# Weight pieces that begin at a different place in their tiles every four pieces

## The chip, the cores and the metric

The kernel runs on one core of a Trainium2 chip. The metric is device time in microseconds (us), median of the runs shown.

## What is computed

The reference is two transformer blocks, one behind the other, on one sequence of 256 tokens with a width of 2048, all in float32. The first block has compressed, selected and windowed attention beside a convolution branch, an output projection and a feed-forward layer with a short convolution. The second has latent attention beside gated linear attention, an output projection, and a gated feed-forward layer, with its scales and shifts from a conditioning vector (adaLN). Cut to its frame:

```python
h = rms_norm(x, mix_norm_g[l])
proj = h @ w_in[l]
...
x = x + jnp.concatenate([attn, conv], axis=-1) @ w_out[l]
h = rms_norm(x, ffn_norm_g[l])
x = x + conv_glu_ffn(h, w_up[l], ffn_conv_w[l], ffn_conv_b[l], w_down[l])
```

Nearly all of the work is activations times weight matrices, with few tokens (256) and some 380 MB of weights that are each used once.

## The kernel before

The weights lie packed in HBM in the order of their use and are cut into 740 pieces, of 128 partitions by up to 1024 elements. `load_raw` brings two pieces at a time into a tile `raw`. Each piece is then split in two, so that TensorE can multiply in its faster float32r form without losing precision: `split_h` (line 456) has ScalarE (ACT) copy the piece to a float32r tile `wh`, the high part; `split_l` (line 463) has VectorE (DVE) write what the rounding left out, `raw - wh`, to a tile `wl`, the low part. There are four buffers of `wh` (LA + 1) and three of `wl` (LA), each 1024 elements long per partition, and both parts begin at the first element of their tile. The activations are held as high and low parts too (`X`, `hid`, `o`, `oh`/`ol`, `ch`/`cl` and others).

`run_group` goes through 119 groups of pieces in a fixed order. In a group of mode `w`, for each of (mostly) four tiles of output columns and each row block k, three matmuls follow each other: `wh` slice with the high activations, the same `wh` slice with the low ones, `wl` slice with the high ones. Here the weights are the stationary operand (128 x 128) and the activations stream through (256 columns; 258 in some matmuls of four groups). A piece gives 24 such matmuls. In a group of mode `x` (114 of the pieces: `vv`, `uv`, `vg`, and the `g` groups, the second block's down projection) the weights stream, with 512 columns, and 128 x 128 of the activations are stationary; a piece gives 12 matmuls. In all there are 16,344 matmuls on weights: 1,368 with 512 columns, 512 with 258, and 14,464 with 256. Each has a weight load of its own.

The work on the side (attention, norms, evacuations, the adaLN sums that are named `ac`) is put between these matmuls by a planner with a model of the engines' time (`tick`, `need`, `Clock`). SP issues the loads, `load_raw` at the end of each tile's `split_l`, when the tile is used up.

Where operands begin: a slice of a weight piece begins a multiple of 128 elements (512 bytes) behind its tile's begin (in `gt` a multiple of 48 elements). `rows` (line 707) puts the activations' rows at a fixed distance of 4 elements (PHASE) behind their tile's begin, with row lengths of 384 (XROW) or 256 elements. In the built program the tiles `wh`, `wl`, `X`, `hid`, `o` and `ch` begin at the same address modulo 512 bytes. So, modulo 512 bytes, the rows of `X`, `hid` and `o` begin 16 bytes behind the weight slices, always. Other activations differ: `ch` has no PHASE and begins 0 bytes behind, `cl` 32 bytes behind, and the heads of `oh` (a tile each, 1,056 bytes apart) begin 16, 48, 80, ... bytes behind, those of `ol` 272, 304, ....

Of the kernel before, what the change touches and what calls it, by code (L numbers as in the profile page):

```python
# [14 lines left out]
F32R = mybir.dt.float32r  # L15
# [13 lines left out]
LA = 3  # L29
# [259 lines left out]
def halves(i, n):  # L289

    return ((0, n // 2), (n // 2, n)) if i == 0 else ((0, n),)


class Engine:


# [76 lines left out]
class Kern:  # L373
# [81 lines left out]

    def split_h(self, i):
        m = MCS[i]
        h = self.wp.tile([128, 1024], F32R, name="wh", bufs=LA + 1)
        for a, b in halves(i, m["len"]):
            self.act(h[:, a:b], self.raws[m["tile"]][:, m["o"] + a:m["o"] + b], AF.Copy)  # L460
        self.hl[i] = h

    def split_l(self, i):
        m = MCS[i]
        n, h = m["len"], self.hl[i]
        l = self.wp.tile([128, 1024], F32R, name="wl", bufs=LA)
        for a, b in halves(i, n):
            self.tt(l[:, a:b], self.raws[m["tile"]][:, m["o"] + a:m["o"] + b], h[:, a:b].bitcast(F32), OP.subtract)
        self.hl[i] = (h, l)
        if i == len(MCS) - 1 or MCS[i + 1]["tile"] != m["tile"]:  # L470
            self.raws.pop(m["tile"])
            self.used = m["tile"] + 1
            self.load_raw(self.used + RAW)
# [1555 lines left out]
```

## Time and profile before

| | |
|---|---|
| median of 3 runs | 2261.15 us (2258.84 to 2265.59) |
| profiled execution | 2265.83 us |
| its span, first to last instruction | 2263.9 us |
| TensorE matmul busy (PE) | 2234.7 us, 99% |
| TensorE weight load busy (PEld) | 2137.7 us, 94% |
| VectorE (DVE) / ScalarE (ACT) busy | 1698.5 us, 75% / 1187.7 us, 52% |
| mean granted TensorE clock | 0.996 |

A matmul's recorded time covers its way through the array, so that two or three overlap: 281 ns for one that has 256 columns, while the next one starts some 115 ns behind it. The busy share therefore says little. What counts is the cadence: the time from one matmul's start to the next one's start. The timeline gives the starts to 10 ns, so that a stretch of many matmuls, divided by their number, gives the cadence to a fraction of a nanosecond.

### The profile page before, as it was taken

The page shows a single profiled execution, that of the slowest core. Times are in us where ns is not written, and L with a number is a line of the kernel's source. Part 1 is how long each engine was busy: PE and PEld are TensorE (multiplying, and loading weights), DVE is VectorE, ACT ScalarE, POOL GpSimd, SP SyncE. Part 2 cuts the span into 40 slices and gives each one's busy share as a digit, 9 for nine tenths or more (in the row PEclk, how much of TensorE's full clock was granted, in tenths as well). Part 3 has the DMA queues.
Part 4 walks back from the last instruction along what each step waited for, and adds up shares of the span by engine and source line. Part 5 has one row for each costly group of instructions (what it writes and reads, how often), then busy time and mean ns, then how long its engine had stood idle before and what let it go on. Part 6 is the DMA issues. An engine that isn't in the chain of part 4 may idle for free.

```text
span 2263.9 us, 42338 instructions
## 1 busy us (share of the span) xinstructions
PE 2234.7 (99%) x17486; PEld 2137.7 (94%) x17486; DVE 1698.5 (75%) x2632; ACT 1187.7 (52%) x1826; POOL 4.9 (0%) x16
## 2 busy tenths in 40 slices
PE   8999999999999999999999999999999999999997
PEld 8998889999999999999999889989998999889996
DVE  7999888898987788888879876577665665544455
ACT  5447776655553355555556664555444444444443
POOL 0000000000000000000000000000000000000000
PEclk9999999999999999999999999999999999999999
DMA  6544325688888787877756644546666665555553
GB/s 242 186 166 159 127 80 193 239 293 301 303 287 308 294 297 284 301 291 290 251 204 225 214 153 148 193 149 215 241 239 231 246 236 192 187 183 171 187 186 130
DMA packets 89089, 499.22 MB, mean 221 GB/s; under 512 B 9904, under 2 KB 12352, under 8 KB 42432
## 3 DMA queue, kind: packets, MB, share of 16 engines
q1 hardware_dynamic: 88896, 496.51, 61.7%
q8 instruction: 137, 2.24, 0.4%
q14 instruction: 56, 0.46, 0.1%
HBM read 494.35 MB, written 2.12 MB: 219 GB/s over the span
## 4 chain that ended last, share of the span: by engine, by line
PE 93%; DVE 4%; ACT 2%; issue 1%; DMA 1%; SPq 0%; DVEq 0%; ACTq 0%
PE ps L305 93%; DVE wl L305 1%; DMA raw<-in_wst_dram 1%; DVE cacc L305 0%; ACT wh L305 0%; DVE og L305 0%; ACT P L305 0%; DVE X L305 0%; ACT X L305 0%; ACT L305 0%; DVE ss L305 0%; DVE blk L305 0%; ACT y L305 0%; ACT vt L305 0%; DVE XT L305 0%
## 5 line engine op out<-in xcount | busy, mean ns | idle before, releaser
L305 PE MATMUL ps<-X,wh 128*128 128x256 f32 (+1 forms) x7680 | 1374.8, 281 | 3.6 <-ACT X L305 2.9
L305 ACT ACTIVATE wh<-raw 128x1024 fp32r<-128x1024 f32 (+2 forms) x741 | 781.5, 1056 | 875.6 <-PE ps L305 798.8
L305 DVE TENSOR_TENSOR wl<-raw,wh 128x1024 fp32r<-128x1024 f32 (+2 forms) x741 | 898.5, 1216 | 451.4 <-PE ps L305 381.3
L305 PEld LDWEIGHTS ps<-X,wh 128*128 128x128 f32 x7680 | 1174.5, 188 | 12.3 <-issue 5.8
L305 PE MATMUL ps<-X,wl 128*128 128x256 f32 (+1 forms) x3840 | 1073.8, 280 | 3.4 <-DVE wl L305 3.4
L305 PEld LDWEIGHTS ps<-X,wl 128*128 128x128 f32 x3840 | 721.3, 188 | 4.0 <-DVE wl L305 4.0
L305 DVE SCALAR_TENSOR_TENSOR ac<-wa,cs,ac 128x512 f32<-128x512 f32 x360 | 269.6, 749 | 6.4
L305 PE MATMUL ps<-hid,wh 128*128 128x256 f32 x1408 | 247.8, 279 | 0.0
L305 PE MATMUL ps<-wh,hid 128*128 128x512 f32 x704 | 220.1, 394 | 0.0
L305 PEld LDWEIGHTS ps<-hid,wh 128*128 128x128 f32 x1408 | 214.1, 188 | 1.2 <-issue 1.2
L305 PE MATMUL ps<-hid,wl 128*128 128x256 f32 x704 | 196.0, 278 | 0.0
L305 PEld LDWEIGHTS ps<-wh,hid 128*128 128x128 f32 x704 | 131.7, 188 | 29.2 <-issue 0.2
L305 PE MATMUL ps<-wl,hid 128*128 128x512 f32 x352 | 138.1, 392 | 0.0
L305 PEld LDWEIGHTS ps<-hid,wl 128*128 128x128 f32 x704 | 132.2, 188 | 0.0
L305 DVE SCALAR_TENSOR_TENSOR cacc<-upad,cat,cacc 128x256 f32<-128x256 f32 x240 | 99.7, 478 | 0.3 <-ACT cacc L305 0.2
L305 PEld LDWEIGHTS ps<-wl,hid 128*128 128x128 f32 x352 | 67.1, 191 | 15.7
L305 DVE SCALAR_TENSOR_TENSOR y<-vt,fv,y 128x256 f32<-128x256 f32 x176 | 73.4, 479 | 0.0
L305 PE MATMUL ps<-wh,X 128*128 128x512 f32 x192 | 62.0, 404 | 0.0
L305 PE MATMUL ps<-o,wh 128*128 128x256 f32 x256 | 48.9, 290 | 1.2 <-ACT o L305 1.1
L305 ACT ACTIVATE y<-ps,fv 128x256 f32<-128x256 f32 x84 | 49.0, 583 | 0.0
L305 ACT ACT_TABLE_LOAD x30 | 38.5, 1283 | 10.8 <-DMA XT<-in_x_dram 4.5
L305 PEld LDWEIGHTS ps<-wh,X 128*128 128x128 f32 x192 | 35.4, 189 | 7.3
(319 smaller groups left out, 1754.8 us busy)
## 6 DMA issues: line engine op xcount, KB each, us to landing
raw<-in_wst_dram SPq DMA_DIRECT2D x363, 1024.0 KB, 4.9
wa<-in_wada_dram SPq DMA_DIRECT2D x176, 512.0 KB, 6.2
wa<-in_wada_dram SPq DMA_DIRECT2D x32, 256.0 KB, 5.5
raw<-in_wst_dram SPq DMA_DIRECT2D x4, 768.0 KB, 4.4
raw<-in_wst_dram SPq DMA_DIRECT2D x4, 512.0 KB, 6.3
B<-dtab SPq DMA_DIRECT2D x8, 256.0 KB, 5.2
out_dram<-og SPq DMA_DIRECT2D x8, 256.0 KB, 2.8
XT<-in_x_dram SPq DMA_DIRECT2D x3, 512.0 KB, 7.5
```

Source lines behind the costliest of these rows:

```text
L305: return f(*x, **k)
```

## The change

A function `places` gives each piece two distances, one for its high part and one for its low part. The tiles `wh` and `wl` become 128 elements longer, and the part begins that many elements behind the tile's begin. Nothing else is changed: not the instructions, their shapes, their order in the program's text, the buffers' number or the loads.

```diff
+def places(i):
+    n = i // 4
+    a, b = (4 * n % 128,) * 2 if n < 64 else (36 * n % 128, 4 * (n * n // 3 + n) % 128)
+    return (a + 2, b + 2) if n % 4 == 3 and n >= 32 else (a, b)
...
     def split_h(self, i):
         m = MCS[i]
-        h = self.wp.tile([128, 1024], F32R, name="wh", bufs=LA + 1)
+        h = self.wp.tile([128, 1024 + 128], F32R, name="wh", bufs=LA + 1)[:, places(i)[0]:]
...
     def split_l(self, i):
...
-        l = self.wp.tile([128, 1024], F32R, name="wl", bufs=LA)
+        l = self.wp.tile([128, 1024 + 128], F32R, name="wl", bufs=LA)[:, places(i)[1]:]
```

Worked out: for the first 256 pieces (n below 64) both parts begin 4n elements (16n bytes) behind, modulo 128 elements, so that all 32 steps of 16 bytes are gone through twice. From then on the high part goes in steps of 36 elements (144 bytes) and the low part in growing ones, so that the two are mostly apart. In every fourth set of four from n = 35 on (152 pieces of the 740) 2 elements (8 bytes) are added to both; all other distances are multiples of 16 bytes.

## Rows read from the trace of the kernel before

**Rows 1.** The page: busy us (share of the span) xinstructions; granted clock in 40 slices.

```profile
PE 2234.7 (99%) x17486; PEld 2137.7 (94%) x17486; DVE 1698.5 (75%) x2632; ACT 1187.7 (52%) x1826; POOL 4.9 (0%) x16
...
PEclk9999999999999999999999999999999999999999
```

**Rows 2.** The page: the chain of work that ended last, share of the span.

```profile
PE 93%; DVE 4%; ACT 2%; issue 1%; DMA 1%; SPq 0%; DVEq 0%; ACTq 0%
```

**Rows 3.** The page's groups: xcount | busy us, mean ns | idle before, releaser.

```profile
L305 PE MATMUL ps<-X,wh 128*128 128x256 f32 (+1 forms) x7680 | 1374.8, 281 | 3.6 <-ACT X L305 2.9
L305 ACT ACTIVATE wh<-raw 128x1024 fp32r<-128x1024 f32 (+2 forms) x741 | 781.5, 1056 | 875.6 <-PE ps L305 798.8
L305 DVE TENSOR_TENSOR wl<-raw,wh 128x1024 fp32r<-128x1024 f32 (+2 forms) x741 | 898.5, 1216 | 451.4 <-PE ps L305 381.3
...
L305 PE MATMUL ps<-wh,hid 128*128 128x512 f32 x704 | 220.1, 394 | 0.0
```

**Rows 4.** Waits: engine, line, releaser: us in total, times, longest us.

```profile
ACT wh L305 <- PE ps L305: 798.8, 525, 5.7
...
DVE wl L305 <- PE ps L305: 381.3, 286, 4.0
```

**Rows 5.** Stretches without side matmuls: us, PE, PEld, DVE, ACT, POOL busy (xcount), clock, DMA.

```profile
410.00:440.00 30.00, 30.00 (x255) 30.00 (x254) 27.32 (x50) 19.52 (x29) 0.00 (x0) 1.00 0.62 228
...
865.00:885.00 20.00, 20.00 (x174) 20.00 (x173) 19.69 (x28) 11.39 (x17) 0.00 (x0) 1.00 0.78 289
...
1010.00:1035.00 25.00, 25.00 (x223) 25.00 (x222) 22.65 (x31) 13.74 (x20) 0.00 (x0) 1.00 0.81 297
1060.00:1080.00 20.00, 20.00 (x174) 20.00 (x173) 18.66 (x25) 10.94 (x16) 0.00 (x0) 1.00 0.76 277
...
1570.00:1600.00 30.00, 30.00 (x255) 30.00 (x254) 19.19 (x23) 12.97 (x17) 0.00 (x0) 1.00 0.73 267
...
1900.00:1930.00 30.00, 30.00 (x260) 30.00 (x259) 14.45 (x14) 12.19 (x14) 0.00 (x0) 1.00 0.57 202
2110.00:2140.00 30.00, 30.00 (x256) 30.00 (x254) 15.29 (x15) 13.27 (x15) 0.00 (x0) 1.00 0.52 179
```

**Rows 6.** The same view, two stretches in which the weights stream (512 columns).

```profile
1940.00:2000.00 60.00, 60.00 (x259) 48.59 (x258) 29.32 (x27) 22.34 (x21) 0.00 (x0) 1.00 0.55 186
2180.00:2250.00 70.00, 70.00 (x311) 57.98 (x310) 37.58 (x37) 30.12 (x38) 0.00 (x0) 1.00 0.44 151
```

**Rows 7.** Timeline of PE at a break by side work: start us, us, what.

```profile
1041.05 0.42 PE L305 MATMUL ps<-ac,vecs 128*32 128x128 f32 x8
```

**Rows 8.** Timeline: first matmuls of group oz0 and, 384 later, of group u0_0.

```profile
349.06 0.28 PE L305 MATMUL ps<-ch,wh 128*128 128x256 f32 x1
...
394.00 0.40 PE L305 MATMUL ps<-X,wh 128*128 128x256 f32 x2
```

**Rows 9.** Timeline, groups o2_1 and o2_2: starts of four runs of 96 matmuls.

```profile
1423.13 0.28 PE L305 MATMUL ps<-oh,wh 128*128 128x256 f32 x1
...
1434.40 0.40 PE L305 MATMUL ps<-X,wh 128*128 128x256 f32 x2
...
1445.80 0.28 PE L305 MATMUL ps<-oh,wh 128*128 128x256 f32 x1
...
1457.07 0.40 PE L305 MATMUL ps<-X,wh 128*128 128x256 f32 x2
```

**Rows 10.** Timeline, group z1: two stretches, of 36 and of 69 matmuls.

```profile
1174.18 0.40 PE L305 MATMUL ps<-X,wh 128*128 128x258 f32 x2
...
1178.34 0.40 PE L305 MATMUL ps<-X,wh 128*128 128x258 f32 x2
...
1187.11 0.42 PE L305 MATMUL ps<-X,wh 128*128 128x258 f32 x2
...
1195.70 0.41 PE L305 MATMUL ps<-X,wh 128*128 128x258 f32 x2
```

**Rows 11.** The tile upad: xcount: ns min/median/max, first and last start.

```profile
L305 DVE SCALAR_TENSOR_TENSOR cacc<-upad,cat,cacc x240: 463/478/485, 45.6 to 308.2; 128x256 f32<-128x256 f32 x120
```

## What the change should do to the time

> **What bounds the kernel.** Read the page first. PE is busy for 2234.7 us, 99% of the span, at the full granted clock (2.4 GHz) in all 40 slices [rows 1], and the chain that ended last is PE for 93% [rows 2]. So no other engine counts on its own; the question is how densely the matmuls follow each other. The two engines that split the weights are not the bound: in the waits ACT stands 798.8 us before `wh` and DVE 381.3 us before `wl`, both for PE to give a buffer free [rows 4]. They run ahead and are held back.
>
> The view on which all else rests is the table by stage [rows 5, 6]: stretches in which only matmuls on weights run. A count there includes the matmuls that were in flight at the opening, so the cadence is the stretch plus one matmul's recorded 0.28 us (0.39 us with 512 columns [rows 3]), over the count. For 256 columns: 30.28/255 = 118.7 ns from 410 us on and again from 1570 us, 20.28/174 = 116.6 from 865 and from 1060, 30.28/260 = 116.5 from 1900, 25.28/223 = 113.4 from 1010, 30.28/256 = 118.3 from 2110 [rows 5]. With 512 columns: 60.39/259 = 233.2 and 70.39/311 = 226.3 [rows 6]. Same shapes, same clock, same relation of the operands' begins (16 bytes), and yet three cadences, each held for tens of us. It doesn't follow the load of DVE, ACT or the DMA: at 410 and at 865 us DVE is busy for 27.32 of 30 and for 19.69 of 20 us, while the 118.3 at 2110 us goes with 15.29 of 30. It changes where the stream is broken: the 113.4 ends at 1041.05 us, where eight short `ac` matmuls of the side work come in [rows 7], and from there it is 116.6. So TensorE's stream has several steady cadences, and a disturbance chooses among them.
>
> The average that the change has to beat: going through the timeline, the undisturbed stretches of 256 columns have 118.7 ns for some 620 us, 116.6 for 750, 113.4 for 36. (620 x 118.7 + 750 x 116.6 + 36 x 113.4) / 1406 = 117.4 ns. One nanosecond more or less on all 14,464 such matmuls is 14.5 us.
>
> **What the change adds and takes away.** No instruction, byte, wait or buffer is added or taken away; the program's order is the same, since the planner's costs depend on shapes. What moves is where `wh` and `wl` begin, and with that the relation to the activations' begin, which was 16 bytes for nearly all matmuls.
>
> *The splits.* ACT's copy (1056 ns) and DVE's subtraction (1216 ns) [rows 3] now write, and DVE reads `wh`, at another begin. The nearest row: the convolution's 31 taps read `upad` at begins one element apart, and take 463 to 485 ns [rows 11]. Taken for nothing; if it were all of those 22 ns, 740 splits would cost DVE 16 us, under the 381.3 us in which it waits for PE [rows 4]. Were that cover gone, the weight load of the next piece would be late by the 22 ns, once in 24 matmuls (0.9 ns each, 13 us in all).
>
> *The matmuls.* Does the begin matter at all? Two places of the trace show matmuls with other relations. Group `oz` has 0 bytes for two of each three matmuls and 32 for the third: 384 matmuls from 349.06 to 394.00 us, 44.94/384 = 117.0 ns [rows 8]. The `o2` groups go through eight heads with relations of 16, 48, 80, ... and 272, 304, ... bytes, and then through 96 matmuls on `X` with 16 bytes: (1434.40 - 1423.13)/96 = 117.4 ns, then 11.40/96 = 118.8, then in the next group 11.27/96 = 117.4 again [rows 9]. Here the cadence changes at once, without a break, as the operand's begin does. So the relation does matter, by about 1 ns, and other relations than 16 bytes gave 117.0 and 117.4, where 16 bytes give 117.4 on average. Put together evenly, (117.0 + 117.4 + 117.4)/3 = 117.3: I take -0.1 ns, or 14,464 x -0.1 = -1.4 us. As bounds I keep the 113.4 ns everywhere, 14,464 x (113.4 - 117.4) = -58 us, and the 118.7 ns everywhere, 14,464 x 1.3 = +19 us. (In the trace only the activations' begin varies, not the weights'; that the relation counts, and not one side alone, is an assumption.)
>
> *The streaming groups.* 1,368 matmuls: 28 of the 114 pieces (the last four groups) have 226.3 ns, nearly all others 233.2, a mean of (28 x 226.3 + 86 x 233.2)/114 = 231.5 ns. All at 233.2 is +2.3 us, all at 226.3 is -7.1 us; taken for nothing.
>
> *The half steps.* In 152 of 740 pieces the begin is 8 bytes off a 16-byte step, which no matmul on weights shows before. The nearest is a row of 258 columns, which ends on such a half step: 4.16 us/36 = 115.6 ns at its quicker cadence [rows 10], against 113.4 for 256 [rows 5]. A column costs (233.2 - 116.6)/256 = 0.46 ns, so two cost 0.9 and 1.3 ns are left over. On 152/740 of 14,464 matmuls, 2,971, that is +4 us; bounds are the steady cadences again, as for any other place. I take a quarter of it, +1 us, since only the first element of each slice is off, and not the length.
>
> Sum: -1.4 + 1 = about -0.5 us on the profiled execution: 2265.83 to 2265.3 (its span of 2263.9 and 1.9 around it). That execution lies 0.2% over the median of 2261.15, so the forecast for the median is 2260.5 us.
>
> *What the skill says.* The Trainium skill, page "TensorE: Matmul & The Clock Gate", section "Step-by-step: what each phase is for", says that PE reads the streaming operand and the weights through two independent SBUF ports, so that loading the next weights takes nothing from the running matmul. By that, in the groups where the weights are stationary, their place would change nothing: 2261 us. The trace doesn't settle it, since only the streaming operand's begin varies in it; it is why a part of the middle case's chance is for no effect at all.
>
> **The rivals.**
> *Other places find the quick cadence.* For it: 113.4 ns exists with these operands [rows 5], and a break can lead into it; a new relation every four pieces is a break without lost time. Against: the runs with other relations [rows 8, 9] didn't fall into it. If a quarter of the matmuls ran at 113.4 and the rest as before, 14,464/4 x 4.0 = -14.5 us: 2247 us.
> *Other places push the stream to 118.7 ns, or worse.* The mechanism is the same, in the other direction: at begins where the two reads get in each other's way the stream settles at a long cadence, and with a new begin every 96 matmuls no good one is kept. For it: a far longer cadence exists, in `z1`, 8.59 us/69 = 124.5 ns beside 115.6 for the same matmuls [rows 10]; 16 bytes may be a good relation among bad ones. Against: again [rows 8, 9], at or below the average. All at 118.7 and 233.2 is +19 + 2.3 us: 2282; a quarter of the matmuls at 124.5 would be 14,464/4 x 7.1 = +26 us, 2287. It decides from a mean of 117.9 ns on. The half steps at their full +4 us only help it.
> *Nothing at all*, because only the activations' begin counts: 2261, inside the forecast.
>
> **How the numbers follow.** A measurement of this kernel tells about 0.3% (6.8 us) from no change, which is 0.47 ns of the mean cadence. Forecast, the mean stays within 0.47 ns: 0.42, of which 0.15 is no effect at all; the three averages in the trace are within 0.4 ns. Faster, 2247: 0.31; slower, 2282: 0.27. The range goes from 2236 (nearly half of the matmuls at 113.4, 0.43 x 58 = 25 us) to 2284 (all at 118.7, and the half steps' 2 us); some 0.1 is left out on each side.
>
> **What would show it.** In the new trace the cadence of the middle of each four pieces, by place: if it falls on the same three values at random, the first case; if single places always have 113.4, the second; if many are over 118.7, the third. The busy times of ACT and DVE for `wh` and `wl`, 781.5 and 898.5 us [rows 3], should stay. I'd be wrong if the pieces with equal relation had different cadences by the begin alone, or if the half steps showed a cadence of their own of 120 ns and more.

## The result, and the profile after

The changed kernel took 2274.64 us (median of 4 runs, 2273.98 to 2276.2), the kernel before beside it 2259.99 (2258.2 to 2265.59): a ratio of 1.0062, with a 95% interval of 1.0043 to 1.0081. It is slower by 14.65 us. That lies inside the predicted range, but beyond the bound of 0.3% that the forecast kept to. The profiled execution after is 2276.2 us (span 2274.2), 10.4 over that of before.

The page after, busy time and chain by engine, against [rows 1, 2]:

```profile
PE 2245.1 (99%) x17486; PEld 2146.7 (94%) x17486; DVE 1698.4 (75%) x2632; ACT 1188.0 (52%) x1826; POOL 4.9 (0%) x16
...
PE 93%; DVE 4%; ACT 2%; DMA 1%; issue 1%; SPq 0%; DVEq 0%; ACTq 0%
```

PE's busy time has grown by 10.4 us, as much as the profiled execution. DVE, ACT, the counts and the chain are unchanged. The groups of after (busy us, mean ns, idle before), against [rows 3]:

```profile
L313 PE MATMUL ps<-X,wh 128*128 128x256 f32 (+1 forms) x7680 | 1381.1, 283 | 2.9 <-ACT X L313 2.6
L313 ACT ACTIVATE wh<-raw 128x1024 fp32r<-128x1024 f32 (+2 forms) x741 | 782.0, 1057 | 886.4 <-PE ps L313 785.4
L313 DVE TENSOR_TENSOR wl<-raw,wh 128x1024 fp32r<-128x1024 f32 (+2 forms) x741 | 898.6, 1216 | 457.9 <-PE ps L313 390.1
```

The splits take what they took (782.0 against 781.5 us, 898.6 against 898.5), and both engines still stand for PE, 785.4 and 390.1 us, about as long as before [rows 4]. So the loss is neither in the splits nor in a wait: it is in the distance from one matmul to the next. That can now be read by place, since every piece of a set of four has the same one. Timeline of after: each row is the first matmul of such a set (start us, us). All sets here are free of side work, and their end is the start of the next set, 96 matmuls later.

```profile
405.11 0.28 PE L313 MATMUL ps<-X,wh 128*128 128x256 f32 x1
...
416.62 0.28 PE L313 MATMUL ps<-X,wh 128*128 128x256 f32 x1
...
428.14 0.28 PE L313 MATMUL ps<-X,wh 128*128 128x256 f32 x1
...
462.23 0.28 PE L313 MATMUL ps<-X,wh 128*128 128x256 f32 x1
...
473.43 0.28 PE L313 MATMUL ps<-X,wh 128*128 128x256 f32 x1
...
565.57 0.28 PE L313 MATMUL ps<-X,wh 128*128 128x256 f32 x1
...
577.09 0.28 PE L313 MATMUL ps<-X,wh 128*128 128x256 f32 x1
...
588.01 0.28 PE L313 MATMUL ps<-X,wh 128*128 128x256 f32 x1
...
783.39 0.28 PE L313 MATMUL ps<-X,wh 128*128 128x256 f32 x1
...
794.91 0.28 PE L313 MATMUL ps<-X,wh 128*128 128x256 f32 x1
...
980.03 0.28 PE L313 MATMUL ps<-X,wh 128*128 128x256 f32 x1
...
990.93 0.28 PE L313 MATMUL ps<-X,wh 128*128 128x256 f32 x1
```

Counting places in steps of 16 bytes behind the tile's begin: place 27 gives (416.62 - 405.11)/96 = 119.9 ns, place 28 (428.14 - 416.62)/96 = 120.0, place 0 (473.43 - 462.23)/96 = 116.7, place 9 (577.09 - 565.57)/96 = 120.0, place 10 (588.01 - 577.09)/96 = 113.8 with the step into it (its later pieces 113.3), place 28 again, 370 us later, 120.0, and the pair of 21 (high) and 5 (low) 113.5. The cadence of a set belongs to its place. Most of the others, read in the same way over the gaps without side work, with the parts alike:

| place (16-byte steps) | ns per matmul of 256 columns |
|---|---|
| 5, 10, 21, 26, and 3.5, 19.5 | 113.3 |
| 0, 16 | 116.7 (place 0 also 113.3 in the first pieces of the kernel and 118.8 in `z2`) |
| 2, 18 | 117.2 |
| 14, 30, 31 | 118.3 |
| 4, 6, 20, 22 | 119.2 to 119.5 |
| 3, 9, 11, 12, 19, 25, 27, 28, and 7.5, 15.5, 23.5, 31.5 | 120.0 |
| 13, 29, and 11.5, 27.5 | 113.3 in one set, 118.3 to 118.9 in another |
| 8, 24 | 116.7 in one set, 118.7 in another |
| 1, 17 | 116.7 in some pieces, 118.2 in others |

Places 16 steps (256 bytes) apart are alike wherever both occur without side work. With the parts at different places, most sets have 117.7 to 118.9, but those whose parts are 256 bytes apart have the cadence of the two alike (5 and 21: 113.3; 4 and 20: 119.2; 12 and 28: 120.0). Of the 626 pieces whose weights are stationary, 86 have a mean under 116 ns and some 175 one of 119 or more.

The sum over these gaps (those between 100 and 140 ns, which leaves out side work): pieces 0 to 255 go from a mean of 117.25 to 117.59 ns, the later ones from 117.63 to 118.08, the streaming groups from 231.4 to 231.6. That is 5,952 x 0.34 + 9,024 x 0.45 + 1,368 x 0.2 = 6.4 us of the 10.4 between the two profiled executions. Most of the rest lies in the first 60 us. Windows of after, columns as in [rows 5] (granted clock third from the right):

```profile
20.00:40.00 20.00, 18.21 (x139) 17.75 (x138) 14.21 (x19) 12.91 (x20) 0.00 (x0) 0.91 0.69 248
40.00:60.00 20.00, 20.00 (x153) 19.05 (x152) 15.94 (x32) 8.80 (x11) 0.00 (x0) 0.91 0.40 151
```

The same windows of before, and a later one:

```profile
20.00:40.00 20.00, 18.94 (x161) 18.68 (x160) 15.66 (x22) 14.90 (x22) 0.00 (x0) 1.00 0.74 265
40.00:60.00 20.00, 20.00 (x165) 19.06 (x164) 17.85 (x36) 8.14 (x12) 0.00 (x0) 1.00 0.40 143
...
1480.00:1500.00 20.00, 16.66 (x118) 15.39 (x117) 13.39 (x23) 9.41 (x18) 0.00 (x0) 0.92 0.42 152
```

After has a mean granted clock of 0.91 from 20 to 60 us, so for a part of it the lower level of 1.2 GHz, and 34 matmuls fewer there, which at 117.5 ns are 4.0 us. Before is at the lower level too at other times, as from 1480 to 1500 us. The experiments below say how far the clock at the start belongs to the change.

### The profile page after: what moved, and what is told of

The parts are those of the page before. It is cut to its first block, busy times and chain, and to the rows that moved or that the text cites. A ratio compares the mean times of both kernels' runs of the same rounds, so it can differ in the third digit from the quotient of the medians.

```text
span 2274.2 us, 42338 instructions
## 1 busy us (share of the span) xinstructions
PE 2245.1 (99%) x17486; PEld 2146.7 (94%) x17486; DVE 1698.4 (75%) x2632; ACT 1188.0 (52%) x1826; POOL 4.9 (0%) x16
## 4 chain that ended last, share of the span: by engine, by line
PE 93%; DVE 4%; ACT 2%; DMA 1%; issue 1%; SPq 0%; DVEq 0%; ACTq 0%
PE ps L313 93%; DVE wl L313 1%; DMA raw<-in_wst_dram 1%; DVE cacc L313 0%; ACT wh L313 0%; DVE og L313 0%; ACT P L313 0%; ACT X L313 0%; ACT L313 0%; DVE X L313 0%; DVE ss L313 0%; DVE blk L313 0%; ACT y L313 0%; DVE XT L313 0%; DVE R L313 0%
## 5 line engine op out<-in xcount | busy, mean ns | idle before, releaser
L313 ACT ACTIVATE wh<-raw 128x1024 fp32r<-128x1024 f32 (+2 forms) x741 | 782.0, 1057 | 886.4 <-PE ps L313 785.4
L313 DVE TENSOR_TENSOR wl<-raw,wh 128x1024 fp32r<-128x1024 f32 (+2 forms) x741 | 898.6, 1216 | 457.9 <-PE ps L313 390.1
```

Of the source, the lines that this page charges most:

```text
L313: return f(*x, **k)
```

## The experiments

The theory after this comparison: where the weight parts begin sets the cadence, place by place, and changing the place costs nothing by itself. The rival: it is the changing that disturbs the stream.

**One place for all, a good one and a bad one.**

```diff
 def places(i):
-    ...
+    return (20, 20)      # first kernel
+    return (12, 12)      # second kernel
```

> All 740 pieces, high and low parts, begin 20 elements (80 bytes) behind their tile's begin; nothing alternates. In the changed kernel the pieces at this place ran at 113.3 ns. Theory 'the place sets the cadence': all 14,464 matmuls of 256 columns on weights run near 113.3 ns, up to 14,464 x (117.4 - 113.3) = 59 us less than the kernel before, so about 2202 to 2212 us (groups whose activations begin elsewhere may keep their own cadence). Rival 'any change of place during the run costs, the place itself doesn't': with one place for all the time is that of the kernel before, 2260 us, with its mix of 113.4, 116.6 and 118.7 ns.

> All pieces, high and low parts, begin 12 elements (48 bytes) behind their tile's begin. In the changed kernel the pieces at this place ran at 120.0 ns. Theory 'the place sets the cadence': 120.0 ns nearly everywhere, 14,464 x (120.0 - 117.4) = 38 us over the kernel before, about 2298 us. Rival 'any change of place during the run costs, the place itself doesn't': 2260 us.

With 20 elements: 2213.93 us, ratio 0.9777 (0.9761 to 0.9794). With 12: 2300.93 us, ratio 1.016 (1.0144 to 1.0176), 3 us over the expected 2298. Windows with 20 elements, one of 256 columns and one of 512:

```profile
410.00:440.00 30.00, 30.00 (x267) 30.00 (x266) 27.66 (x50) 21.76 (x34) 0.00 (x0) 1.00 0.74 266
...
2130.00:2190.00 60.00, 60.00 (x266) 49.67 (x266) 34.45 (x34) 28.93 (x36) 0.00 (x0) 1.00 0.48 166
```

The same kind with 12 elements, 256 columns:

```profile
410.00:440.00 30.00, 30.00 (x252) 30.00 (x251) 27.96 (x52) 18.77 (x30) 0.00 (x0) 1.00 0.62 221
1570.00:1600.00 30.00, 30.00 (x252) 30.00 (x251) 21.89 (x38) 16.25 (x23) 0.00 (x0) 1.00 0.60 209
```

30.28/267 = 113.4 ns against 30.28/252 = 120.2 in the stretch that had 118.7 before [rows 5], and 60.39/266 = 227.0 for streaming weights. The clock is 1.00 in all of them. The rival falls: nothing changes place here, and the two kernels are 87 us apart, with the same instructions. The estimate of 2202 to 2212 us was 2 us too low at its upper end, since groups with other activations or with 258 columns keep another cadence (`oz`, `z0`, `z1`, `f0_0`, `uq` have 117.7 to 118.2).

A second thing is in the spread: four runs with 12 elements lie within 1.5 us and four with 20 within 3.5, but seven of the kernel before within 8.4 (2261.74 to 2270.11).

**The relation, or the weights' own begin.** The prediction assumed that the relation of the weights' begin to the activations' counts. Here the weights stay at 0, and the activations are moved instead, to the relation that 20 elements for the weights give.

```diff
 def places(i):
-    ...
+    return (0, 0)
...
-    def rows(self, pool, name, parts, skip=PHASE):
+    def rows(self, pool, name, parts, skip=112):
...
-        t = pool.tile([128, skip + sum(n * w for n, w in parts)], F32R, name=name)
+        t = pool.tile([128, skip + 20 + sum(n * w for n, w in parts)], F32R, name=name)
```

> The weight parts begin at their tile's first element, as in the kernel before; instead the rows of the activations X, o and hid begin 448 bytes behind their tile's begin in place of 16, so that modulo 512 bytes a weight slice begins 64 bytes behind the activations, the relation that 20 elements for the weights give. Theory 'the relation of the two begins counts' (an assumption of the prediction): 113.3 ns nearly everywhere, 2202 to 2212 us, equal to the run in which the weights begin 20 elements behind. Rival 'the weights' own begin counts': 117.4 ns on average as in the kernel before, 2260 us. Third, 'the activations' own begin counts': some other cadence, unlike both.

2227.56 us (2220.14 to 2232.62, the widest spread of all these kernels), ratio 0.9829 (0.9799 to 0.986): neither of the first two theories. Its windows, two with 256 columns and one with 512:

```profile
410.00:440.00 30.00, 30.00 (x257) 30.00 (x256) 27.32 (x48) 20.59 (x32) 0.00 (x0) 1.00 0.68 253
1010.00:1035.00 25.00, 25.00 (x222) 24.68 (x222) 22.77 (x33) 11.66 (x14) 0.00 (x0) 1.00 0.82 291
...
2145.00:2205.00 60.00, 60.00 (x263) 49.22 (x263) 34.44 (x34) 28.74 (x36) 0.00 (x0) 1.00 0.51 174
```

117.8 ns in the first, 25.28/222 = 113.9 in the second (by the starts of a set of 96 matmuls 113.3, as in most of the kernel), 229.6 with 512 columns. So moving the activations works too, and the same relation often brings the same 113.3; but it has a second cadence at 117.8, which 20 elements for the weights did not show in any set on `X` or `hid` without side work. `oz`, whose activations were not moved, stays at 117.1 ns, what it has in [rows 8], while with 20 elements it has 117.8.

The complement: both operands moved by the same 80 bytes, so that the relation is that of before.

```diff
 def places(i):
-    ...
+    return (20, 20)
...
-    def rows(self, pool, name, parts, skip=PHASE):
+    def rows(self, pool, name, parts, skip=PHASE + 20):
...
-        t = pool.tile([128, skip + sum(n * w for n, w in parts)], F32R, name=name)
+        t = pool.tile([128, skip + 108 + sum(n * w for n, w in parts)], F32R, name=name)
```

> Weights begin 20 elements (80 bytes) behind their tile's begin, and the rows of X, hid and o 24 elements in place of 4: both operands are moved by 80 bytes, and the relation of their begins is that of the kernel before. Theory 'the relation alone counts': the mix of 113.4, 116.7 and 118.7 ns of the kernel before, 2258 to 2270 us. Rival 'the weights' own place counts': 113.3 ns, 2214 us. Third, from the run that moved the activations alone and got 113.3 in some stretches and 117.8 in others: relation and own place both count; a cadence that is neither, between 113.3 and 120 ns, 2214 to 2300 us.

2298.54 us, ratio 1.0171 (1.0156 to 1.0187). Its windows, two with 256 columns and one with 512:

```profile
410.00:440.00 30.00, 30.00 (x252) 30.00 (x252) 28.07 (x51) 18.87 (x30) 0.00 (x0) 1.00 0.61 223
...
1850.00:1880.00 30.00, 30.00 (x258) 30.00 (x258) 19.30 (x21) 12.70 (x15) 0.00 (x0) 1.00 0.67 230
...
2215.00:2275.00 60.00, 60.00 (x256) 48.27 (x255) 33.59 (x34) 28.20 (x36) 0.00 (x0) 1.00 0.47 158
```

120.2 and 30.28/258 = 117.4 ns, and 60.39/256 = 235.9 with 512 columns, longer than any of [rows 6]. With the relation of before none of the three cadences of before returns with 256 columns. The relation alone doesn't decide, nor does the weights' own begin alone (the same 20 elements gave 113.4): each operand's begin counts, together with the other's.

**Two parts at two places.** High parts at 20, low parts 256 bytes behind that, or 80 bytes behind.

```diff
 def places(i):
-    ...
+    return (20, 84)      # first kernel
+    return (20, 40)      # second kernel
```

> All high parts begin 20 elements (80 bytes) behind their tile's begin, all low parts 84 elements (336 bytes); modulo 256 bytes the two are alike. In the changed kernel the pieces with this pair ran at 113.3 ns with 256 columns and at 226.7 with 512, without an exception. Theory 'the place sets the cadence': 14,464 x 4.1 = 59 us and 1,368 x (231.4 - 226.7) = 6 us less than before, about 2195 to 2208 us. If the distance between high and low part counts on its own, it is another time than with 20 for both. Rival 'any change of place during the run costs': 2260 us.

> High parts begin 20 elements behind, low parts 40, all the time. Each of the two places alone, for both parts alike, gives 113.3 ns. Theory A 'each part has a cadence of its own, by its own relation to the activations': 113.3 ns, 2214 us. Theory B 'the distance between high and low part counts, since the load of one part's weights runs beside the matmul on the other': 117.8 ns as nearly all pieces with parts 5 places apart in the changed kernel, 2214 + 14,464 x 4.4 = 64 us less what the other groups keep, 2265 to 2278 us.

With 84: 2215.32 us, ratio 0.9782 (0.9766 to 0.9798), like 20 for both; 256 bytes make no difference. (It is 7 us over the expected 2208, for the groups that keep another cadence, as with 20 for both.) With 40: 2272.28 us, ratio 1.0055 (1.0042 to 1.0069), although 40 alone, as 20 alone, gives 113.3. Windows with 20 and 40:

```profile
60.00:75.00 15.00, 15.00 (x135) 15.00 (x134) 12.62 (x22) 7.12 (x8) 0.00 (x0) 1.00 0.44 149
...
410.00:440.00 30.00, 30.00 (x257) 30.00 (x257) 27.54 (x50) 19.82 (x30) 0.00 (x0) 1.00 0.62 229
...
1060.00:1080.00 20.00, 20.00 (x172) 20.00 (x172) 17.93 (x30) 11.94 (x20) 0.00 (x0) 1.00 0.75 271
```

30.28/257 = 117.8 and 20.28/172 = 117.9, as in most of the kernel. So the distance from high to low part counts too, as theory B has it: with 20 for both parts no set on `X` without side work had 117.8. But the distance does not force that cadence: from 60 to 75 us it is 15.28/135 = 113.2, and 25 of the first 40 pieces have about 113.3. 117.8 is what the changed kernel has in most of its second part, and why single good places among the two parts don't help there.

**Changing among good places only.**

```diff
 def places(i):
-    ...
+    return ((20, 84, 40, 104)[i // 4 % 4],) * 2
```

> As in the changed kernel the begin changes every four pieces, high and low parts alike, but only among 20, 84, 40 and 104 elements, the four whole 16-byte places at which the changed kernel showed 113.3 ns. Theory 'the place sets the cadence, changing it costs nothing': about 113.3 ns after each change, the time of the kernel with 20 for all pieces, 2214 us, at most 5 us more. Rival 'each change of place disturbs the stream': 185 changes add their share of the changed kernel's 14.65 us, so well over 2225 us.

2220.85 us, ratio 0.9831 (0.9817 to 0.9844): some 39 us less than before, with 184 changes of place in it. It is 7 us over 20 elements for all, 2 more than the first theory allowed, and under what the rival asked for. (The two were measured beside different runs of before, with medians of 2259.41 and 2263.52; their profiled executions, 2220.15 and 2212.71, are 7.4 us apart.) Timeline, first matmuls of four sets in a row, each at another place:

```profile
396.80 0.28 PE L309 MATMUL ps<-X,wh 128*128 128x256 f32 x1
...
407.68 0.28 PE L309 MATMUL ps<-X,wh 128*128 128x256 f32 x1
...
418.56 0.28 PE L309 MATMUL ps<-X,wh 128*128 128x256 f32 x1
...
429.44 0.28 PE L309 MATMUL ps<-X,wh 128*128 128x256 f32 x1
```

10.88/96 = 113.3 ns each, with three changes of place among them: a change costs nothing. The 7 us lie mostly where the weights stream: there 20 and 84 elements have 226.7 ns, 40 and 104 have 233.3; the mean of 230.5 against 227.0 is 1,368 x 3.5 = 4.8 us.

**Without the half steps.**

```diff
-    return (a + 2, b + 2) if n % 4 == 3 and n >= 32 else (a, b)
+    return a, b
```

> The changed kernel without the half steps: 152 pieces begin on a whole 16-byte place in place of 8 bytes behind one. Rival, the prediction's bound 'half steps cost 4 us of their own': 2270.5 us or less. Theory 'only the place's cadence counts, and the half steps had both good (113.3 ns at 3.5, 11.5, 19.5, 27.5) and bad ones (120.0 at 7.5, 15.5, 23.5, 31.5)': their pieces averaged 117.8 ns, the others 117.9; among the first 64 sets the whole places instead are 120.0 four times and 116.7 to 118.3 four times, some 2 us more: 2275 to 2279 us, within 0.2% of the changed kernel.

2276.21 us, ratio 1.0074 (1.0062 to 1.0087), 1.6 us over the changed kernel's 2274.64, measured at another time; that says no more than "no gain". The bound of 4 us for the half steps is gone. In the changed kernel their pieces have a mean of 117.8 ns, the others 117.9; without them the same pieces have 118.8.

**Each part of the change alone, and the change again.**

```diff
     a, b = (4 * n % 128,) * 2 if n < 64 else (36 * n % 128, 4 * (n * n // 3 + n) % 128)
+    if n >= 64:
+        return 0, 0
```

This is the first part alone; the second part alone has `if n < 64:` there. In both the tiles stay 128 elements longer than before.

> Only the change's first part: pieces 0 to 255 go through the 32 places, high and low alike; from piece 256 on both begin at the first element as in the kernel before. Theory 'the time is the sum of the places' cadences': the profiles put 5,952 x (117.6 - 117.25) = 2 us on these pieces beside some 4 us at the start; over the median of before, which lies below its profiled execution, 4 to 8 us: 2264 to 2268 us. Rival 'all of the loss is at the start, the clock in the first 60 us': the full 12 to 15 us are here, 2272 to 2275 us, and none is in the second part.

> Only the change's second part: pieces 0 to 255 begin at the first element, from piece 256 on each part has its own place. Theory 'the time is the sum of the places' cadences': 9,024 x (118.1 - 117.6) = 4 us over the profiled execution of before and 6 to 10 us over its median: 2266 to 2270 us; both parts' differences add up to that of the changed kernel within 3 us. Rival 'all of the loss is at the start': 2260 us.

> The changed kernel once more, for its cadences and its clock. Theory 'the place sets the cadence': each place shows the cadence of the first profile to 0.2 ns (113.3 at 5, 10, 21 and 26 steps, 120.0 at 3, 11, 12, 19, 27, 28), and 2274 to 2276 us, while the clock in the first 60 us may be another. Rival 'a disturbance chooses among the cadences' (the prediction's reading of before): other cadences at the same places. Rival 'the clock at the start belongs to the change': again some 0.90 from 20 to 60 us and at 1515 us.

Beside the same runs of before (2260.12): the first part 2268.12, ratio 1.004 (1.0027 to 1.0053); the second part 2266.88, ratio 1.0037 (1.0025 to 1.0049); both together 2273.74, ratio 1.0063 (1.0051 to 1.0075). The differences, 8.0 and 6.8 us, add up to 14.8 against 13.6 measured. So the loss is not all at the start: it is spread over the whole kernel, as the places are.

The second profile of the changed kernel, timeline, sets at places 28, 10 and (21, 5):

```profile
415.90 0.28 PE L313 MATMUL ps<-X,wh 128*128 128x256 f32 x1
...
427.42 0.28 PE L313 MATMUL ps<-X,wh 128*128 128x256 f32 x1
...
576.37 0.28 PE L313 MATMUL ps<-X,wh 128*128 128x256 f32 x1
...
587.29 0.28 PE L313 MATMUL ps<-X,wh 128*128 128x256 f32 x1
...
979.90 0.28 PE L313 MATMUL ps<-X,wh 128*128 128x256 f32 x1
...
990.80 0.28 PE L313 MATMUL ps<-X,wh 128*128 128x256 f32 x1
```

120.0, 113.8 and 113.5 ns, as in the first; of the 740 pieces 691 have the mean cadence of the first profile to 0.2 ns. At some places it is otherwise. The set at place 29 begins at 794.91 us in the first profile (above), and there it ends, with the begin of the next set, at

```profile
805.80 0.28 PE L313 MATMUL ps<-X,wh 128*128 128x256 f32 x1
```

In the second profile the same set begins and ends at

```profile
794.35 0.28 PE L313 MATMUL ps<-X,wh 128*128 128x256 f32 x1
...
805.71 0.28 PE L313 MATMUL ps<-X,wh 128*128 128x256 f32 x1
```

10.89/96 = 113.4 ns against 11.36/96 = 118.3, with the same program. Place 0 is another such place. The first part alone has place 0 from piece 256 on, as the kernel before has, and these are its windows there:

```profile
865.00:885.00 20.00, 20.00 (x179) 20.00 (x178) 18.27 (x26) 12.10 (x18) 0.00 (x0) 1.00 0.84 310
...
1570.00:1600.00 30.00, 30.00 (x256) 30.00 (x255) 18.15 (x21) 12.96 (x17) 0.00 (x0) 1.00 0.68 247
```

20.28/179 = 113.3 ns from 865 us on, where the kernel before had 116.6 with the same operands [rows 5]; from 1570 on 118.3 against 118.7. The mean over pieces 256 and later is 117.30 ns here and 117.63 in the profile of before: 9,024 x 0.33 = 3.0 us between two executions with the same places, though of kernels whose tiles differ in length.

The clock. In the second part alone the first 256 pieces begin at 0, as in the kernel before. Its windows:

```profile
20.00:40.00 20.00, 20.00 (x170) 19.95 (x170) 15.57 (x21) 15.48 (x22) 0.00 (x0) 0.99 0.76 276
40.00:60.00 20.00, 20.00 (x153) 19.07 (x152) 17.24 (x35) 7.57 (x11) 0.00 (x0) 0.91 0.34 124
```

From 40 to 60 us it has 0.91, as after the change, although all pieces up to there begin at 0. So the lower clock there does not need the changed places. For 20 to 40 us it says nothing, with 0.99; but the kernel with all weights at 0 and the activations moved has 0.92 there, and those with 20 and with 12 elements for all have 1.00. What remains open is the length of the tiles: all twelve profiles of kernels with the longer tiles have 0.90 or 0.91 from 40 to 60 us, and the one profile of before has 1.00. Against the tiles speaks that the mean clock of whole executions varies in both: it is 0.994 to 0.996 in 27 runs of before, and 0.996 in its profiled one. The five runs of the second measurement of the changed kernel have 0.993 (2276.18 and 2276.15 us), 0.995 (2272.01) and 0.996 (2273.74 and 2271.5), so some 2 to 5 us between them; the runs of before show no such link to their time. What lets the clock fall in some executions and not in others was not tried.

## Why the prediction was wrong

**What bounds the kernel** was right: the density of PE's stream. (The full clock in all 40 slices was read too far: a 9 stands for 90% or more, and before has 0.92 from 1480 to 1500 us.) Nothing in the splits or the waits moved, and a gain or loss in the cadence went to the end almost whole (20 elements for all: a mean of 114.1 instead of 117.5 ns, 14,976 x 3.4 = 51 us, and 1,368 x 4.4 = 6 us where the weights stream; the profiled executions are 53 us apart).

**The splits** were right at zero, and **the half steps** nearly (+1 us forecast, no loss measured).

**The matmuls: the step that failed.** The prediction took -0.1 ns as the mean effect of other places, from three averages, 117.0, 117.4 and 117.4 [rows 8, 9], "put together evenly". The changed kernel goes through 32 whole places, and then through pairs of them, and these reach from 113.3 to 120.0 ns; the three that the trace of before showed all lie in the middle. The bad places outweigh the good ones, so that the mean is 117.9 instead of the 117.3 of the prediction. An average over three values of unknown spread was treated as the average over all places, and two of the three were the same activations met twice. Even a single one of them was no constant. Group `oz` in the second part alone, with the weights at 0 as before, and then in the kernel before:

```profile
352.00:390.00 38.00, 38.00 (x319) 38.00 (x319) 31.36 (x52) 23.76 (x39) 0.00 (x0) 1.00 0.58 194
```

```profile
352.00:390.00 38.00, 38.00 (x327) 38.00 (x326) 31.39 (x53) 24.69 (x40) 0.00 (x0) 1.00 0.56 191
```

38.28/319 = 120.0 ns against 38.28/327 = 117.1.

In the profiled executions the mean rose by 0.41 ns (117.48 to 117.89), so 6 us, just inside the bound of 0.47. Two things carried the result over it. One is the some 4 us in the first 60 us of the profiled execution, for which the prediction has no term. The other is the base: the profiled execution of before lies 5.8 us above the median of the runs beside the changed kernel, that of after 1.6 above its own. The prediction scaled its sum with the profile, but the cadence in it seems to be on the high side of what executions show: place 0 gave 113.3 in one execution where it gave 116.6 in another. Against that other execution the same pieces differ by 118.08 - 117.30 = 0.78 ns, 7.0 us, and that fits the 6.8 measured for the second part alone. It accounts for 3.0 of the 5.8 us; the rest of the base was not traced.

**The assumption about the relation** was half right. Moving the activations to the relation of 20 elements brought 113.3 ns in most of the kernel, so that the relation matters; moving both left it as it was and still brought 117.4 and 120.2. That is one of the two marks that the prediction named for being wrong: equal relation, different cadence. The other, half steps with 120 ns and more, came too (7.5, 15.5, 23.5, 31.5), and meant nothing, since 3.5 and 19.5 have 113.3.

**The reading of before,** "a disturbance chooses among them", holds at most for place 0 and a few others (29, and 20 with 40 elements) and was wrongly made general. There the cadence differs within an execution or between two of them. At most places there is one cadence, whatever DVE, ACT and the DMA do beside it.

**The rivals.** The first needed good places to be found at random and forecast 2247; good places exist and are fixed, but only 86 of the pieces had them. The second, "push the stream to 118.7 ns, or worse", is what happened to the time, though not because changing keeps the stream from a good place, since a change costs nothing: its point of decision, a mean of 117.9 ns, is where the mean came out, and its own 2282 us, for all pieces at 118.7, was 7 us more than the time. The worst cadence is 120.0, and not the 124.5 of `z1`, which place 0 has with 258 columns.

**No effect at all** is excluded: moving only the weights, by 80 bytes, took 50 us. The Trainium skill, page "TensorE: Matmul & The Clock Gate", section "Step-by-step: what each phase is for", says that weights and streaming operand are read through two independent ports, so that loading the next weights takes nothing from the running matmul. What the prediction made of that, a time that stays at 2261 us, does not agree with the runs: the matmul's cadence goes from 113.4 to 120.2 ns with the weights' begin alone. Why is not shown. The recorded weight loads of `X` and `wh` do not tell the two apart (their means are 188 ns with 20 elements and 189 with 12), and whether the two reads meet, and where, no run here shows.

## What to carry to other kernels

Where TensorE is busy for 99% of the span, measure the cadence of its matmuls by operand, and try the operands' begins in the buffer as a parameter of its own: one constant, 20 elements for `wh` and `wl`, gives 2213.93 us here, 2.2% less than before, with no instruction changed. Keep the parts that follow each other alike modulo 256 bytes. An effect that differs from place to place can't be forecast from the mean of the two or three places that a trace happens to show; measure one place at a time, and then take the best, instead of a mixture.

## What the runs showed of the hardware

- In these runs, with float32r operands, an own weight load for each matmul and 256 columns, the cadence at the full clock takes few values: 113.3, 116.7, 117.2 to 117.8, 118.3 to 118.9, 119.2 and 120.0 ns. With 512 columns 226.7, 228.3 to 229.3, 231 to 233.6, 234.5 and 236.7. Nothing under 113.3 and 226.7 was seen in any undisturbed set.
- The cadence depends on where the weights begin, modulo 256 bytes, and, together with that, on where the activations begin; moving both by 80 bytes is not neutral. Neighbouring 16-byte steps differ by up to 6.7 ns (9 and 10: 120.0 and 113.3), half steps have values of their own.
- What is best for stationary weights need not be best for streaming ones: places 10 and 26 give 113.3 ns with 256 columns and 233.3 with 512; 5 and 21 give 113.3 and 226.7.
- Some places have two or three cadences (0, 8, 13, 24, 29), and which one holds can differ between two executions of the same program (29: 113.4 and 118.3 ns). Whether that makes the kernel before's spread of 7 to 9 us, against 1.5 and 3.5 with 12 and 20 elements, is not shown: place 0 differs by 3.0 us between two profiles, but the five runs of the first part alone, with the same place 0 from piece 256 on, lie within 2.3 us.
